# Moving a sums' buffer by 64 bytes and laying each row tile's activations side by side, in a hybrid decoder layer

## The chip, the cores and the metric

The kernel runs on one core of a Trainium2 chip. The metric is device time in microseconds (us); several runs of a kernel are taken and their median counts, and less is better. One more execution is recorded by the hardware profiler, and all rows of a profile come from that one.

## What is computed

One decoder layer on 1024 tokens of width 1024, all in float32:

```
h = rms_norm(x, mix_norm);  z = h @ w_in             # q, k, v, gates of two groups of heads
o_gla = gated linear attention, chunks of 64          # 4 heads
o_swa = sliding-window attention (128) with sinks     # 8 query heads, 2 kv heads
x  = x + concat([o_gla, o_swa]) @ w_out
h2 = rms_norm(x, ffn_norm)
u  = causal_depthwise_conv3(h2 @ w_up)                # 1024 -> 2 * 2816
a, b = split(u);  return x + (silu(a) * b) @ w_down   # 2816 -> 1024
```

## The kernel before

**Precision.** A float32 matmul is made of three fp32r matmuls. Each operand is split into a high part (index 0) and a rest (index 1), and the products high x high, high x rest and rest x high are summed in PSUM (`PASSES`). Every matmul is one weight load (128 columns of the stationary operand, `lhsT`) and one stream of up to 512 columns of the moving operand (`rhs`).

**Stages.** Tokens are cut into NT = 8 row tiles of 128, the model width into KD = 8 slices of 128. (1) `norm1` normalises a row tile and transposes it into the buffer `big` (`tr_hi` and `tr_lo` write the high part and the rest). (2) `dense` multiplies a row tile of `big` (stationary) by a block of w_in (moving): units dq, dk, dv, dg, dr, with the attention's small matmuls between them. (3) The gated outputs are written back into `big` (`gate_tr`), and `dense` multiplies them by w_out (do). (4) `norm2` normalises again; row tiles 0 to 3 go into `big` as before, and for tiles 4 to 7 `norm2_sums` forms sums and differences with tiles 0 to 3, which go into `big` and into the sums' buffer `ex`. (5) The gated MLP: DFF = 2816 is cut into 22 chunks of 128. For each chunk `product` does seven products of twelve matmuls each (a scheme after Strassen and Winograd, seven half-size products in place of eight): the stationary operand is a 128x128 piece of the chunk's w_up operand (A11w, A12w, S1w to S4w, A22w), the moving operand is 512 tokens of an activation, which `b_operand` picks: B11, B21, B22 and T1 lie in `big`, T2, T3 and T4 in `ex`. Between two products stands one `down_pair` (L1024), six matmuls of 512 columns for w_down, whose result VectorE adds to `acc` (L1028). At the end `last_row` does the last two chunks' share of w_down.

**Names in the profile.** `fb<-ex,S2w` at L843 is a product into a PSUM bank fb with moving operand in `ex` and stationary operand S2w; `gb<-` are those of chunk 0; `dn_P<-dw,dg` at L1024 is a `down_pair`.

**Order.** A list of times (`at`, `at_us`) sorts the steps once when the program is built; TensorE, VectorE, ScalarE and GpSimd then run their own rows in that order. An operand of `product` is made two products ahead by ScalarE (high part) and by GpSimd or VectorE (rest).

**Where buffers lie.** SBUF gives each of the 128 partitions the same byte addresses. Pools are stacked: from below `base` (`big`, raw weights, small things), upon it `gl` (attention), and once that is closed `acc`, then `ex`, then `pn` or `ff`; from above the nine weight slots of 4096 bytes (`slot_tile`), which hold all stationary operands of the products, and both operands of `down_pair`. Start addresses in bytes, from the program's allocation, with what is left modulo 256 (below: the phase):

| buffer | start before | phase before | phase after |
|---|---|---|---|
| weight slots (lowest 192384, steps of 4096) | 192384 | 128 | 128 |
| `big` | 1152 | 128 | 128 |
| `ex` | 112448 | 64 | 128 |
| A11w and A12w of chunk 1 (a pool above `ex`, not slots) | 178240, 182336 | 64 | 128 |
| `acc` | 79680 | 64 | 128 |
| kw, ident, qo, vg (from above) | | 0, 128, 128, 128 | the same |
| the attention's tiles in `gl` | | various | each 64 more |

Indices inside `big` and `ex` move by multiples of 512 bytes, so they keep the phase.

Of the kernel before, what the change touches and what calls it, by code (L numbers as in the profile page):

```python
# [9 lines left out]
F32 = mybir.dt.float32  # L10
F32R = mybir.dt.float32r
# [6 lines left out]
P = 128  # L18
T = 1024
D = 1024  # L20
NT = T // P
KD = D // P
# [12 lines left out]
def hymba_layer_kernel(ctx, tc, x, mix_norm, w_in, w_alpha2, b_alpha, gla_norm,  # L35
# [3 lines left out]
    act, dve, pool, pe, sp = nc.scalar, nc.vector, nc.gpsimd, nc.tensor, nc.sync  # L39
# [10 lines left out]
    base = ctx.enter_context(tc.tile_pool(name="base", bufs=1))  # L50
# [4 lines left out]
    def bank(name):  # L55
        ps["n"] += 1
        if "f" in ps:
            return ps["f"][2 + ps["n"] % 2]

        for start, which in (("n2pt_6", "b"), ("do1_7", "a"), ("n2pt_3", "a")):  # L60
            if name.startswith(start):
                return ps[which].tile([P, 512], F32, tag="b", name=name)
        return ps["ab"[ps["n"] % 2]].tile([P, 512], F32, tag="b", name=name)

    big = base.tile([P, 2, KD, 2, 4, P], F32R, name="big")

    def rows(t, ks, r):
        return big[:, t // 4, ks, r, t % 4, :]

    RAW_BUFS, K4, K2, N_WARM = 3, 6, 5, 5  # L70

# [23 lines left out]
    def split(src, hi, lo, eng=None, hi_eng=None):  # L95
        if hi_eng is None:
            act.copy(hi, src)  # L97
        else:
            hi_eng.tensor_copy(hi, src)
        (eng or pool).tensor_sub(lo, src, hi.bitcast(F32))  # L100
# [89 lines left out]
    def norm1_tr(t, i):  # L190
        tr_hi(t, i, xts["h", t], "n1")

    def norm1_lo(t, i):
        tr_lo(t, i, "n1")
# [32 lines left out]
    def norm2_sums(t):  # L227

        i, ex, pn = t - 4, fin["ex"], fin["pn"]
        p0, p1 = fin["pb", t]  # L230

        def put(src, hi, lo):
            split(src, hi, lo, dve)

        def extra(n):
            return ex[:, n, :, 0, i, :], ex[:, n, :, 1, i, :]

        def own(ks):
            return rows(t, ks, 0), rows(t, ks, 1)

        b12 = pn.tile([P, 4, P], F32, tag="b12", name=f"b12_{t}", bufs=1)
        b11, b21 = ([rows(i, ks, r).bitcast(F32) for r in range(2)] for ks in (slice(0, 4), slice(4, 8)))
        act.copy(b12, p0)
        put(p1, *own(slice(4, 8)))
        dve.tensor_sub(p0, p0, b11[0])
        dve.tensor_sub(p0, p0, b11[1])
        put(p0, *own(slice(0, 4)))
        dve.tensor_sub(p1, p1, b12)
        put(p1, *extra(1))
        dve.tensor_add(p1, p1, b11[0])  # L250
        dve.tensor_add(p1, p1, b11[1])
        put(p1, *extra(0))
        dve.tensor_sub(p0, b21[0], p1)
        dve.tensor_add(p0, p0, b21[1])
        put(p0, *extra(2))

    trs = {}

    def tr_hi(t, q, h, tag):
        pt = bank(f"{tag}pt_{t}_{q}")  # L260
        for k in range(4):
            c = (q * 4 + k) * P
            pe.transpose(pt[:, k * P:(k + 1) * P], h[:, c:c + P], ident)
        trs[tag, t, q] = pt.rearrange("p (k c) -> p k c", k=4)
        act.copy(rows(t, slice(q * 4, q * 4 + 4), 0), trs[tag, t, q])

    def tr_lo(t, q, tag):
        hi, lo = (rows(t, slice(q * 4, q * 4 + 4), r) for r in range(2))
        dve.tensor_sub(lo, trs[tag, t, q], hi.bitcast(F32))

    def norm_tr(t, h, tag):
        for q in range(2):
            tr_hi(t, q, h, tag)
            tr_lo(t, q, tag)


    blocks = {}
# [45 lines left out]
    def dense(t, ws, n, name):  # L323
        pb = bank(name)
        for k in range(KD):
            for i, (ra, rb) in enumerate(PASSES):
                pe.matmul(pb[:, :n], lhsT=rows(t, k, ra), rhs=ws[k][:, rb, :n],  # L327
                          start=(k == 0 and i == 0), stop=(k == KD - 1 and i == 2))
        return pb

# [299 lines left out]
    def gate_tr(t, gs):  # L630
        pb = bank(f"ogt{t}")
        for h in range(4):
            pe.transpose(pb[:, h * P:(h + 1) * P], gs[:, h * P:(h + 1) * P], ident)
        pv = pb.rearrange("p (h c) -> p h c", h=4)
        hi, lo = (rows(t, slice(0, 4), r) for r in range(2))
        act.activation(hi, pv, AF.Copy, scale=glan)
        dve.scalar_tensor_tensor(lo, pv, glan, hi.bitcast(F32), op0=ALU.mult, op1=ALU.subtract)
        src = qo[:, t, :].rearrange("p (j c) -> p j c", j=4)
        hi, lo = (rows(t, slice(4, 8), r) for r in range(2))
        split(src, hi, lo)  # L640


    fin = {}
# [19 lines left out]
    def open_norm2():  # L663
        st.close()
        w_late["pool"] = swp.enter_context(tc.tile_pool(name="wb", bufs=1, side="right"))
        xp = ctx.enter_context(tc.tile_pool(name="xp", bufs=1))
        fin["ex"] = xp.tile([P, 3, 4, 2, 4, P], F32R, name="ex")
        fin["sn"] = ExitStack()
        pn = fin["pn"] = fin["sn"].enter_context(tc.tile_pool(name="pn", bufs=1))
        ffn = fin["ffn"] = pn.tile([P, D], F32, name="ffn")  # L670
        sp.dma_start(ffn, ffn_norm.partition_broadcast(P).rearrange("p o d -> p (o d)"))
        fin["s1"] = pn.tile([P, 4, P], F32, name="s1_0")
# [18 lines left out]
    psb = {}  # L691
# [18 lines left out]
    def unit_q_part(t, k0, k1):  # L710
        if k0 == 0:
            psb["q", t] = bank(f"dq{t}")
        pb = psb["q", t]
        for k in range(k0, k1):

            for i, (ra, rb) in enumerate(((0, 0), (1, 0), (0, 1))):
                pe.matmul(pb, lhsT=rows(t, k, ra), rhs=blocks["q"][k][:, rb, :],  # L717
                          start=(k == 0 and i == 0), stop=(k == KD - 1 and i == 2))

    def q_done(t):  # L720
# [2 lines left out]
    def unit_q(t):  # L723
        q_post(t, dense(t, blocks["q"], 512, f"dq{t}"))

    def unit_k(t):
        kvl_post(t, dense(t, blocks["k"], 272, f"dk{t}"))

    def unit_v(t):
        act.activation(vg[0][:, t, :], dense(t, blocks["v"], 512, f"dv{t}"), AF.Copy, scale=row_scale(t))  # L730
# [78 lines left out]

    def b_operand(name, k, r):  # L810
        ex = fin["ex"]
        return {"B11": big[:, 0, k, r], "B21": big[:, 0, 4 + k, r],
                "B22": big[:, 1, 4 + k, r], "T1": big[:, 1, k, r],
                "T2": ex[:, 0, k, r], "T3": ex[:, 1, k, r], "T4": ex[:, 2, k, r]}[name]

    PROD = {"P1": ("A11", "B11"), "P2": ("A12", "B21"), "P3": ("S4", "B22"), "P4": ("A22", "T4"),
            "P5": ("S1", "T1"), "P6": ("S2", "T2"), "P7": ("S3", "T3")}
# [12 lines left out]
    def product(ch, name):  # L830
        an, bn = PROD[name]
        w = blocks["u", ch, an]
        onto = ONTO.get(name)
        if ch == 0 and name == "P3":
            onto = None
        if onto is None:
            psb[name, ch] = up_bank(ch, {"P1": 0, "P2": 1, "P3": 2, "P5": 2 if ch else 3}[name])
        pb = psb[name, ch] = psb[onto or name, ch]
        steps = [(k, ra, rb) for k in range(4) for ra, rb in PASSES]
        if ch == 0:  # L840
            steps.sort(key=lambda step: step[2])
        for i, (k, ra, rb) in enumerate(steps):
            pe.matmul(pb, lhsT=w[:, ra, k, :], rhs=b_operand(bn, k, rb),  # L843
                      start=(onto is None and i == 0), stop=(i == 11), skip_group_check=onto is not None)
# [50 lines left out]
        act.copy(dst, pb)  # L895

    def save_edge(ch, key, pb):
        e = psb[key, ch] = fin["ff"].tile([P, 2], F32, tag="e", name=f"{key}_{ch}", bufs=2)
        act.copy(e, pb[:, 510:512])

    def c11(ch):
# [196 lines left out]
    for c in halves:  # L1098
        split(mix_row[:, c], mix_hl[0][0:1, c], mix_hl[1][0:1, c], dve)
        pb = bank(f"mix{len(mix_ps)}")  # L1100
# [4 lines left out]
    def mix_copy():  # L1105
        for c, pb in zip(halves, mix_ps):
# [3 lines left out]
    TU = TO + 16.0  # L1110
    FIRST = ((norm1_mul, 0, 0), (q_hi, 0), (q_lo, 0, pool), (norm1_mul, 0, 1), (warm_up, 2), (norm1_tr, 0, 0),
             (norm1_lo, 0, 0), (q_hi, 1), (q_lo, 1, dve), (warm_up, 1), (norm1_tr, 0, 1), (warm_up, 2), (unit_q_part, 0, 0, 2), (q_hi, 2), (q_lo, 2, pool),
             (q_hi, 3), (norm1_mul, 1, 0), (q_lo, 3, dve), (unit_q_part, 0, 2, 3), (norm1_tr, 1, 0),
             (norm1_lo, 1, 0), (unit_q_part, 0, 3, 4), (q_hi, 4), (q_lo, 4, pool), (norm1_lo, 0, 1),
             (norm1_mul, 1, 1), (unit_q_part, 1, 0, 3), (q_hi, 5), (q_lo, 5, pool), (norm1_tr, 1, 1),
             (unit_q_part, 1, 3, 4), (norm1_lo, 1, 1), (q_hi, 6), (q_lo, 6, dve), (q_hi, 7), (q_lo, 7, pool),
# [80 lines left out]
    at(TO + 8.006, mark)  # L1197
    at(TO - 0.05, open_acc)
    at(TO + 1.35, open_norm2)
    def at_us(us, f, *a):  # L1200
        at(TU + us / 5.2, f, *a)
# [18 lines left out]
    for ch, i, name in order:  # L1220
# [7 lines left out]
        if ch < 2 or (ch, i) == (2, 0):  # L1228
            n = 0
        elif ch < L - 1 or (ch, i) == (L - 1, 0):  # L1230
            n = 1
        else:
            n = 2
# [24 lines left out]
    for p in range(NPAIR):  # L1258
        for k in range(7):

            n = 7 * p + k - 2
# [51 lines left out]
```

## Time and profile before

| | |
|---|---|
| runs | median 1039.2 us of 3 (1038.97 to 1039.4) |
| profiled execution, its own time | 1039.1 us |
| its span, first to last instruction | 1037.4 us |
| granted TensorE clock over the span | 1.000 |
| TensorE matmuls | busy 99% of the span, 4976 instructions |
| VectorE, GpSimd, ScalarE | busy 76%, 60%, 46% of the span |

How to read it: the span is what the rows add up to; 1.7 us of the execution lie around it. A group's row gives line, engine, operation, output<-inputs, shape and count, then busy time and the mean duration of one. Matmuls are pipelined: the duration of one runs from its start to its modelled end and is longer than the distance from one start to the next, so what a matmul costs in a dense stretch is read from the starts in the timeline.

### The profile page before, as it was taken

To read this page: it belongs to the slowest core of one execution; us is meant where nothing else is said; L and a number is where in the kernel's file an instruction comes from. 1 tells how busy PE (TensorE), PEld (TensorE's weight loads), DVE (VectorE), ACT (ScalarE), POOL (GpSimd) and SP (SyncE) were. 2 spreads that over 40 slices of the span, in tenths; PEclk is the share of its full clock that TensorE was granted. 3 is DMA by queue.
4 is the path that set the end of the run, shared out by engine and by line. 5 is a ranking of instruction groups with operands and counts; after the bars stand their busy time and mean duration, and the time that the engine had idled before them with its cause. 6 is when DMAs were issued, how large, how long until landed. Compare 5 with 4: busy or idle time off the path is not lost.

```text
span 1037.4 us, 13921 instructions
## 1 busy us (share of the span) xinstructions
PE 1030.0 (99%) x4976; PEld 849.3 (82%) x4976; DVE 793.4 (76%) x1332; ACT 480.6 (46%) x988; POOL 618.4 (60%) x510
## 2 busy tenths in 40 slices
PE   9999999999999999999999999999999999999998
PEld 6899887888888888888888888888888888888887
DVE  6776667755131699887979899897979798998976
ACT  5627655445340446554444445444444444454441
POOL 4592132325550205867868787877778787978750
PEclk9999999999999999999999999999999999999999
DMA  6152113002044202112120111222121211121104
GB/s 217 61 154 62 45 50 93 21 1 82 1 122 163 61 1 82 41 41 82 41 81 26 57 45 57 61 62 62 41 82 41 62 41 47 55 62 61 41 21 162
DMA packets 67502, 67.13 MB, mean 65 GB/s; under 512 B 4648, under 2 KB 52201, under 8 KB 67434
## 3 DMA queue, kind: packets, MB, share of 16 engines
q1 hardware_dynamic: 63448, 61.27, 18.9%
q10 hardware_dynamic: 3986, 4.99, 2.0%
q8 instruction: 39, 0.64, 0.2%
q14 instruction: 29, 0.24, 0.1%
HBM read 57.33 MB, written 4.19 MB: 59 GB/s over the span
## 4 chain that ended last, share of the span: by engine, by line
PE 97%; DMA 1%; DVE 1%; ACT 0%; issue 0%; POOL 0%; DVEq 0%; ACTq 0%; SPq 0%
PE fb L843 39%; PE dn_P L1024 18%; PE do L327 8%; PE dr L327 4%; PE dg L327 4%; PE dv L327 4%; PE dq L327 3%; PE dk L327 2%; PE gb L843 2%; PE dq L717 1%; PE pv L500 1%; PE fb L1053 1%; PE dl L1053 1%; PE go L610 1%; PE ga L601 1%; PE sc L453 1%
## 5 line engine op out<-in xcount | busy, mean ns | idle before, releaser
L1028 DVE TENSOR_TENSOR acc<-acc,dn_P 128x1024 f32<-128x1024 f32 x140 | 169.9, 1215 | 61.5 <-PE dn_P L1024 60.3
L1024 PE MATMUL dn_P<-dw,dg 128*128 128x512 f32 x840 | 214.0, 390 | 0.0
L1024 PEld LDWEIGHTS dn_P<-dw,dg 128*128 128x128 f32 x840 | 157.6, 188 | 34.5
L327 PE MATMUL do<-wow,big 128*128 128x512 f32 x384 | 90.9, 393 | 0.0
L100 POOL TENSOR_TENSOR dw<-dn,dw 128x512 fp32r<-128x512 f32 x50 | 68.8, 1376 | 25.3 <-ACT dw L97 24.1
L327 PEld LDWEIGHTS do<-wow,big 128*128 128x128 f32 x384 | 71.1, 188 | 14.4
L895 ACT COPY ca<-fb 128x512 f32<-128x512 f32 x62 | 36.3, 586 | 68.2 <-PE fb L843 68.2
L843 PE MATMUL fb<-ex,S2w 128*128 128x512 f32 x252 | 62.5, 394 | 0.0
L843 PE MATMUL fb<-ex,S3w 128*128 128x512 f32 x252 | 62.5, 394 | 0.0
L850 DVE SCALAR_TENSOR_TENSOR ua<-fb,cc,ua 128x511 f32<-128x511 f32 x84 | 62.2, 741 | 0.3
L843 PE MATMUL fb<-ex,A22w 128*128 128x512 f32 x252 | 62.2, 394 | 0.0
L843 PE MATMUL fb<-big,A11w 128*128 128x512 f32 x252 | 61.2, 389 | 0.0
L843 PE MATMUL fb<-big,S1w 128*128 128x512 f32 x252 | 61.1, 389 | 0.0
L843 PE MATMUL fb<-big,S4w 128*128 128x512 f32 x252 | 61.1, 389 | 0.0
L843 PE MATMUL fb<-big,A12w 128*128 128x512 f32 x252 | 60.9, 390 | 0.0
L843 PEld LDWEIGHTS fb<-ex,S2w 128*128 128x128 f32 x252 | 47.2, 187 | 11.3
L843 PEld LDWEIGHTS fb<-ex,A22w 128*128 128x128 f32 x252 | 47.2, 187 | 11.3
L843 PEld LDWEIGHTS fb<-ex,S3w 128*128 128x128 f32 x252 | 47.2, 187 | 11.3
L843 PEld LDWEIGHTS fb<-big,S1w 128*128 128x128 f32 x252 | 47.3, 188 | 10.0
L843 PEld LDWEIGHTS fb<-big,A11w 128*128 128x128 f32 x252 | 47.3, 188 | 10.0
L843 PEld LDWEIGHTS fb<-big,S4w 128*128 128x128 f32 x252 | 47.3, 188 | 10.0
L843 PEld LDWEIGHTS fb<-big,A12w 128*128 128x128 f32 x252 | 47.2, 188 | 9.8
(432 smaller groups left out, 2392.1 us busy)
## 6 DMA issues: line engine op xcount, KB each, us to landing
up<-in_w_up_dram SPq DMA_DIRECT2D x44, 512.0 KB, 3.8
dn<-in_w_down_dram SPq DMA_DIRECT2D x22, 512.0 KB, 3.5
acc<-in_x_dram SPq DMA_DIRECT2D x8, 512.0 KB, 6.5
out_dram<-acc SPq DMA_DIRECT2D x15, 256.0 KB, 2.0
xt<-in_x_dram SPq DMA_DIRECT2D x7, 512.0 KB, 3.2
vraw<-in_w_in_dram SPq DMA_DIRECT2D x4, 512.0 KB, 3.9
graw<-in_w_in_dram SPq DMA_DIRECT2D x4, 512.0 KB, 3.7
qt<-qt ACTq DMA_DIRECT2D x16, 128.0 KB, 2.2
```

The lines of the kernel that those rows point to most:

```text
L100: (eng or pool).tensor_sub(lo, src, hi.bitcast(F32))
L327: pe.matmul(pb[:, :n], lhsT=rows(t, k, ra), rhs=ws[k][:, rb, :n], start=(k == 0 and i == 0), stop=(k == KD - 1 and i == 2))
L453: pe.matmul(pbs[-1][:, j % 2, :], lhsT=ql[:, g, qc], rhs=kt[:, g, kc], start=False, stop=True)
L500: pe.matmul(pbs[i][HALF[g]], lhsT=vv[rows, t - 1 + b, HALF[g]], rhs=rhs[rows, :, HALF[i]], start=start, stop=stop)
L601: pe.matmul(pb[:, pr * 256:(pr + 1) * 256], lhsT=gqt[t][:, pr, :], rhs=qbd[t % 2][:, pr], start=(pr == 0), stop=(pr == 1))
L610: pe.matmul(pb[:, h * P:(h + 1) * P], lhsT=asb[:, h, :], rhs=v[:, h * P:(h + 1) * P], start=(h == 0), stop=(t == 0 and h == 3))
L843: pe.matmul(pb, lhsT=w[:, ra, k, :], rhs=b_operand(bn, k, rb), start=(onto is None and i == 0), stop=(i == 11), skip_group_check=onto is n ...
L850: dve.scalar_tensor_tensor(dst, src, w, dst, op0=ALU.mult, op1=ALU.add)
L895: act.copy(dst, pb)
L1024: pe.matmul(pb[:, i], lhsT=g[:, ra, c:c + P], rhs=w[:, rb, :], start=(onto is None and n == 0), stop=(n == 2), skip_group_check=onto is no ...
L1028: dve.tensor_add(acc, acc, pb)
L1053: pe.matmul(pb[:, c0:c1], lhsT=g[:, ra, (t % 4) * P:(t % 4 + 1) * P], rhs=w[:, rb, c0:c1], start=(ch == NCH - 2 and i == 0), stop=(ch == N ...
```

## The change

Two things, and no instruction is added, removed or moved: both programs issue the same instructions on every engine in the same order. What differs is addresses and access patterns.

First, the two tiles of `save_edge` (`e`, [128, 2], the last two token rows of a half) come from `base` and no longer from `ff`. `base` grows by two buffers of 32 bytes, and all that is stacked above it starts 64 bytes higher; in `ff` the tiles behind the old place of `e` stay where they were.

Second, the index order of `big` and of `ex`. Before, the 512 tokens of four row tiles lay side by side for each slice k and part r: the moving operand of a product was one run of 2048 bytes in each partition, and the eight slices of one row tile lay 4096 bytes apart, high part and rest 2048 bytes apart. Afterwards a row tile's slices and parts lie side by side: the moving operand of a product is four runs of 512 bytes, 8192 bytes apart in `big` and 4096 bytes apart in `ex`; a row tile's slices are 1024 bytes apart, high part and rest 512. A stationary operand taken from `big` is one run of 512 bytes either way.

```diff
-    big = base.tile([P, 2, KD, 2, 4, P], F32R, name="big")
-
-    def rows(t, ks, r):
-        return big[:, t // 4, ks, r, t % 4, :]
+    big = base.tile([P, NT, KD, 2, P], F32R, name="big")
...
-        act.copy(rows(t, slice(q * 4, q * 4 + 4), 0), trs[tag, t, q])
+        act.copy(big[:, t, q * 4:q * 4 + 4, 0, :], trs[tag, t, q])
...
-                pe.matmul(pb[:, :n], lhsT=rows(t, k, ra), rhs=ws[k][:, rb, :n],
+                pe.matmul(pb[:, :n], lhsT=big[:, t, k, ra, :], rhs=ws[k][:, rb, :n],
...
-        fin["ex"] = xp.tile([P, 3, 4, 2, 4, P], F32R, name="ex")
+        fin["ex"] = xp.tile([P, 3, 4, 4, 2, P], F32R, name="ex")
...
-        return {"B11": big[:, 0, k, r], "B21": big[:, 0, 4 + k, r],
-                "B22": big[:, 1, 4 + k, r], "T1": big[:, 1, k, r],
-                "T2": ex[:, 0, k, r], "T3": ex[:, 1, k, r], "T4": ex[:, 2, k, r]}[name]
+        return {"B11": big[:, 0:4, k, r, :], "B21": big[:, 0:4, 4 + k, r, :],
+                "B22": big[:, 4:8, 4 + k, r, :], "T1": big[:, 4:8, k, r, :],
+                "T2": ex[:, 0, :, k, r, :], "T3": ex[:, 1, :, k, r, :],
+                "T4": ex[:, 2, :, k, r, :]}[name]
...
-        e = psb[key, ch] = fin["ff"].tile([P, 2], F32, tag="e", name=f"{key}_{ch}", bufs=2)
+        e = psb[key, ch] = base.tile([P, 2], F32, tag="e", name=f"{key}_{ch}", bufs=2)
```

The other lines of the diff (`norm2_sums`, `tr_lo`, `gate_tr`, `unit_q_part`) only write the new indices.

More of the change, by code (lines that the diff above doesn't have):

```diff
@@ L230, in norm2_sums, with put @@
         p0, p1 = fin["pb", t]
[L232 to L239, printed above, removed]
+        def put(src, dst):
+            split(src, dst[:, :, 0, :], dst[:, :, 1, :], dve)
         b12 = pn.tile([P, 4, P], F32, tag="b12", name=f"b12_{t}", bufs=1)
-        b11, b21 = ([rows(i, ks, r).bitcast(F32) for r in range(2)] for ks in (slice(0, 4), slice(4, 8)))
+        b11, b21 = big[:, i, 0:4].bitcast(F32), big[:, i, 4:8].bitcast(F32)
         act.copy(b12, p0)
[L244 to L247, printed above, removed]
+        put(p1, big[:, t, 4:8])
+        dve.tensor_sub(p0, p0, b11[:, :, 0, :])
+        dve.tensor_sub(p0, p0, b11[:, :, 1, :])
+        put(p0, big[:, t, 0:4])
         dve.tensor_sub(p1, p1, b12)
[L249 to L255, printed above, removed]
+        put(p1, ex[:, 1, i])
+        dve.tensor_add(p1, p1, b11[:, :, 0, :])
+        dve.tensor_add(p1, p1, b11[:, :, 1, :])
+        put(p1, ex[:, 0, i])
+        dve.tensor_sub(p0, b21[:, :, 0, :], p1)
+        dve.tensor_add(p0, p0, b21[:, :, 1, :])
+        put(p0, ex[:, 2, i])
     trs = {}
@@ L264, in tr_hi @@
         trs[tag, t, q] = pt.rearrange("p (k c) -> p k c", k=4)
-        act.copy(rows(t, slice(q * 4, q * 4 + 4), 0), trs[tag, t, q])
+        act.copy(big[:, t, q * 4:q * 4 + 4, 0, :], trs[tag, t, q])
     def tr_lo(t, q, tag):
-        hi, lo = (rows(t, slice(q * 4, q * 4 + 4), r) for r in range(2))
+        hi, lo = big[:, t, q * 4:q * 4 + 4, 0, :], big[:, t, q * 4:q * 4 + 4, 1, :]
         dve.tensor_sub(lo, trs[tag, t, q], hi.bitcast(F32))
@@ L634, in gate_tr @@
         pv = pb.rearrange("p (h c) -> p h c", h=4)
-        hi, lo = (rows(t, slice(0, 4), r) for r in range(2))
+        hi, lo = big[:, t, 0:4, 0, :], big[:, t, 0:4, 1, :]
         act.activation(hi, pv, AF.Copy, scale=glan)
@@ L638, in gate_tr @@
         src = qo[:, t, :].rearrange("p (j c) -> p j c", j=4)
-        hi, lo = (rows(t, slice(4, 8), r) for r in range(2))
+        hi, lo = big[:, t, 4:8, 0, :], big[:, t, 4:8, 1, :]
         split(src, hi, lo)
@@ L716, in unit_q_part @@
             for i, (ra, rb) in enumerate(((0, 0), (1, 0), (0, 1))):
-                pe.matmul(pb, lhsT=rows(t, k, ra), rhs=blocks["q"][k][:, rb, :],
+                pe.matmul(pb, lhsT=big[:, t, k, ra, :], rhs=blocks["q"][k][:, rb, :],
                           start=(k == 0 and i == 0), stop=(k == KD - 1 and i == 2))
```

## The prediction

> **What bounds the kernel now.** I read the page from the top: busy shares, then the chain that ended last, then the costliest groups.
>
> ```profile
> span 1037.4 us, 13921 instructions
> PE 1030.0 (99%) x4976; PEld 849.3 (82%) x4976; DVE 793.4 (76%) x1332; ACT 480.6 (46%) x988; POOL 618.4 (60%) x510
> ...
> PE 97%; DMA 1%; DVE 1%; ACT 0%; issue 0%; POOL 0%; DVEq 0%; ACTq 0%; SPq 0%
> ...
> L1028 DVE TENSOR_TENSOR acc<-acc,dn_P 128x1024 f32<-128x1024 f32 x140 | 169.9, 1215 | 61.5 <-PE dn_P L1024 60.3
> L1024 PE MATMUL dn_P<-dw,dg 128*128 128x512 f32 x840 | 214.0, 390 | 0.0
> ...
> L843 PE MATMUL fb<-ex,S2w 128*128 128x512 f32 x252 | 62.5, 394 | 0.0
> L843 PE MATMUL fb<-ex,S3w 128*128 128x512 f32 x252 | 62.5, 394 | 0.0
> ...
> L843 PE MATMUL fb<-ex,A22w 128*128 128x512 f32 x252 | 62.2, 394 | 0.0
> L843 PE MATMUL fb<-big,A11w 128*128 128x512 f32 x252 | 61.2, 389 | 0.0
> L843 PE MATMUL fb<-big,S1w 128*128 128x512 f32 x252 | 61.1, 389 | 0.0
> ...
> L843 PE MATMUL fb<-big,A12w 128*128 128x512 f32 x252 | 60.9, 390 | 0.0
> ```
>
> TensorE is the bound: 97% of the chain, and the product groups have no idle time ahead of them (the last column is 0.0). What one matmul costs is therefore what the kernel costs. The rows to look at twice are those of L843: the same shape, the same nine slots for the stationary operands, and yet 394 ns where the moving operand lies in `ex` and 389 to 390 where it lies in `big`. The medians, and the twelve further matmuls of chunk 0 (gb), say the same, in a view of line 843 with minimum, median and maximum:
>
> ```profile
> L843 PE MATMUL fb<-ex,S2w x252: 393/394/398, 414.2 to 995.1; 128*128 128x512 f32 x126
> L843 PE MATMUL fb<-big,S1w x252: 388/389/398, 420.7 to 1008.9; 128*128 128x512 f32 x126
> L843 PE MATMUL gb<-ex,A22w x12: 394/394/394, 423.4 to 426.0; 128*128 128x512 f32 x12
> ```
>
> The spread is a few ns over 580 us, so this is no contention with other engines, which would vary; it belongs to the addresses. The timeline of TensorE gives the price from start to start (columns: start, length, engine, group):
>
> ```profile
> 701.18 2.96 PE L843 MATMUL fb<-ex,S2w 128*128 128x512 f32 x12
> 703.98 1.54 PE L1024 MATMUL dn_P<-dw,dg 128*128 128x512 f32 x6
> 705.36 2.88 PE L843 MATMUL fb<-big,S1w 128*128 128x512 f32 x12
> 708.08 1.52 PE L1024 MATMUL dn_P<-dw,dg 128*128 128x512 f32 x6
> 709.44 2.96 PE L843 MATMUL fb<-ex,S3w 128*128 128x512 f32 x12
> ...
> 730.04 2.96 PE L843 MATMUL fb<-ex,S2w 128*128 128x512 f32 x12
> ```
>
> A product from `ex` takes 703.98 - 701.18 = 2.80 us, one from `big` 708.08 - 705.36 = 2.72: 233.3 and 226.7 ns a matmul. The unit behind a product from `ex` takes 705.36 - 703.98 = 1.38, the one behind `big` 709.44 - 708.08 = 1.36: after `ex` the stream needs some matmuls to get back into step. The whole cycle of a chunk, from S2w to S2w, is 730.04 - 701.18 = 28.86 us, and seven products and seven units at 2.72 and 1.36 would be 28.56: the difference of 0.30 is three times (0.08 + 0.02), so nothing else is lost there.
>
> Is it the phase? `ex` starts at 64 modulo 256 and everything else in these rows at 128, so two explanations fit: the phase, or something else about `ex`. One place tells them apart. The operands A11w and A12w of chunk 1 don't lie in slots but at phase 64, while their moving operand is `big`:
>
> ```profile
> 399.48 2.46 PE L843 MATMUL fb<-big,A11w 128*128 128x512 f32 x10
> 401.77 1.08 PE L843 MATMUL gb<-big,A12w 128*128 128x512 f32 x4
> ```
>
> and, among the matmuls that write fb between 399 and 407 us, with minimum, median and maximum:
>
> ```profile
> L843 PE MATMUL fb<-big,A12w x12: 388/394/477, 403.7 to 406.3; 128*128 128x512 f32 x12
> L843 PE MATMUL fb<-big,A11w x11: 388/392/397, 399.5 to 402.7; 128*128 128x512 f32 x11
> ```
>
> (401.77 - 399.48) / 10 = 229 ns, medians 392 and 394: with the stationary operand 64 bytes off and `ex` not involved, matmuls are slow as well. So it is the difference between the two operands' phases, and I take equal phases for worth 226.7.
>
> **The change, part by part.**
>
> *`ex` at phase 128.* Products from `ex`: 3 x 252 + 3 x 12 = 792 matmuls, 66 products. At 0.08 each that is 66 x 0.08 = 5.28 us. The getting back into step, 0.02, falls away behind each of them but some four in chunks 0 and 1 where one product from `ex` follows another: 62 x 0.02 = 1.24. All of it lies on TensorE with no idle time, so all of it counts. Sum 6.5.
>
> *A11w and A12w of chunk 1 at phase 128.* 24 matmuls at 229 - 226.7 = 2.3 ns: 0.06 us, lost in rounding.
>
> *The moving operand in four runs.* All 7 x 252 + 7 x 12 = 1848 product matmuls now read 4 x 128 elements with three jumps. No fp32r matmul of this kernel does so; the nearest are plain float32 ones, 256 columns in four runs of 64 (L500) against 256 in one run (L420):
>
> ```profile
> L500 PE MATMUL pv<-pt,vv x120: 376/379/431, 119.0 to 253.8; 128*64 128x256 f32 x64, 64*64 64x256 f32 x56
> ...
> L420 PE MATMUL za<-wa,gt x16: 377/379/382, 79.4 to 114.4; 128*128 128x256 f32 x16
> ```
>
> Both have a median of 379: three jumps cost nothing there. I take 0, since jumps of 4096 and 8192 bytes leave the phase as it is and each run is two whole periods of 256. The row is weak, as a plain float32 matmul takes in its columns more slowly. The other end: if every matmul lost in the jumps what a foreign phase costs it, 6.7 ns, it would be 1848 x 6.7 = 12.3 us. A gain I exclude: the undisturbed rows of `big`, dn_P and the rest all stand at 389 to 390.
>
> *Row tiles side by side, as stationary operands.* `dense` reads runs of 512 bytes, before and after, at multiples of 512; only the distance from one to the next falls, from 2048 or more to 512. The weight loads of dn_P already have 512-byte neighbours, those of do are spread out, and both take 188 ns:
>
> ```profile
> L1024 PEld LDWEIGHTS dn_P<-dw,dg 128*128 128x128 f32 x840 | 157.6, 188 | 34.5
> ...
> L327 PEld LDWEIGHTS do<-wow,big 128*128 128x128 f32 x384 | 71.1, 188 | 14.4
> ```
>
> So 0. ScalarE's and VectorE's writes into `big` and `ex` stay four runs of 512 bytes at another distance; they are off the chain, and I cost them at 0 under TensorE's cover.
>
> *64 bytes for the attention's tiles.* In the first 394 us `dense` does not run quite at its best:
>
> ```profile
> L327 PE MATMUL do<-wow,big 128*128 128x512 f32 x384 | 90.9, 393 | 0.0
> ...
> L327 PE MATMUL dg<-gw,big 128*128 128x512 f32 x192 | 47.0, 399 | 1.0 <-ACT vg L730 1.0
> L327 PE MATMUL dv<-vw,big 128*128 128x512 f32 x192 | 46.5, 395 | 0.0
> L327 PE MATMUL dr<-rw,big 128*128 128x512 f32 x192 | 46.5, 396 | 0.0
> ```
>
> Above 389 that is 384 x 4 + 192 x (10 + 6 + 7) ns = 6.0 us, waits and getting into step after each small matmul. The phases of `big` and the slots don't move; those of the small matmuls between them do, together, so each keeps its neighbours in `gl` in phase. I take 0; a shift of a sixth of the 6.0, 1 us, either way goes into the range.
>
> *What comes due earlier.* The chunk shrinks to 28.56 us, and the other engines must keep up. Busy time in 440 us of this stage (PE, PEld, DVE, ACT, POOL):
>
> ```profile
> 560.00:1000.00 440.00, 440.00 (x1923) 360.20 (x1922) 388.91 (x482) 210.07 (x357) 341.72 (x251) 1.00 0.18 54
> ```
>
> VectorE goes from 388.91 / 440 = 88% to 388.91 / 435.4 = 89%, and the L1028 row shows it waiting 60.3 us for dn_P: it stays behind TensorE.
>
> The sum is 6.5 us against the profiled execution: 1039.1 - 6.5 = 1032.6. The median of the runs lies 0.1 above that execution: 1032.7.
>
> **The rivals.**
>
> *The jumps cost* (slower). In every product each matmul loses one step of 6.7 ns at its jumps, and `ex` gains what it gains: 1032.7 + 12.3 = 1045.0. It decides from 6.5 us / 1848 = 3.5 ns a matmul on. For it: no fp32r row with jumps exists, and a stream that falls out of step by 64 bytes pays. Against it: L500 beside L420, and jumps by whole periods. 0.13. With 2.4 to 4.6 ns the two parts would cancel within 2.1 us: 0.02, and with less the kernel is still faster: 0.02.
>
> *The phase is not what makes `ex` slow* (no change): 1039.2. For it: every row at 394 has `ex` in it, and the chunk 1 rows are only 24 matmuls, some next to transposes. The Trainium skill, "TensorE: Matmul & The Clock Gate", section "Step-by-step: what each phase is for", says that the moving operand and the weight load have read ports of their own, so that loading weights takes nothing from the running matmul; by that rule the distance of two addresses could not matter, and the time would stay at 1039.2. The trace disagrees in that 2.80 and 2.72 differ by the operands' places alone. 0.07.
>
> *VectorE or GpSimd becomes the bound.* Excluded by the 88% and 341.72 / 440 = 78% above as long as the order stays.
>
> **How the numbers follow.** Forecast 0.76, its own range 1031.5 (6.5 + 0.1, and the 1 us in `dense`) to 1034.0 (without the 1.24, or with that 1 us). Jumps that cost: 0.13 slower, 0.02 cancelling, 0.02 at some 1036. Phase without effect: 0.07. This measurement tells about 0.2%, 2.1 us, from no change: faster 0.76 + 0.02 = 0.78, same 0.02 + 0.07 = 0.09, slower 0.13. The range of 8 in 10 reaches from 1031.5 to the cases without effect, 1039.4, and leaves the slower ones out.
>
> **What would show it.** Right: the `ex` groups of L843 at 389, products of 2.72 and units of 1.36 throughout, S2w to S2w 28.56, a span of 1030.9, `dense` as before. If the `big` groups rise above 389, the jumps cost; if `ex` stays at 394 at phase 128, the phase was not the cause; if the gain is there but `dense` has moved, it is the shift of `gl`. The forecast is wrong as soon as jumps cost 3.5 ns.

## The result and the profile after

The kernel after takes 1032.99 us (median of 4, 1032.79 to 1033.26) against 1039.28 before (median of 4): a ratio of 0.994, 95% interval 0.9923 to 0.9957. The forecast was 1032.7. The profiled execution took 1033.08 us, its span is 1031.4. Its page, head and costliest groups (line numbers are 8 to 9 lower than before):

```profile
span 1031.4 us, 13921 instructions
PE 1023.9 (99%) x4976; PEld 849.5 (82%) x4976; DVE 795.6 (77%) x1332; ACT 480.7 (47%) x988; POOL 618.3 (60%) x510
...
L1016 PE MATMUL dn_P<-dw,dg 128*128 128x512 f32 x840 | 212.9, 389 | 0.0
...
L318 PE MATMUL do<-wow,big 128*128 128x512 f32 x384 | 90.9, 393 | 0.0
...
L835 PE MATMUL fb<-big,A12w 128*128 128x512 f32 x252 | 60.9, 390 | 0.2 <-DVE ua L842 0.2
...
L835 PE MATMUL fb<-big,S1w 128*128 128x512 f32 x252 | 61.0, 389 | 0.0
L835 PE MATMUL fb<-ex,S3w 128*128 128x512 f32 x252 | 60.9, 389 | 0.0
```

Every fb group of products now stands at 389 to 390, `ex` and `big` alike; dn_P has come down from 390 to 389, and `do` is where it was. The timeline of TensorE over one chunk:

```profile
698.20 2.88 PE L835 MATMUL fb<-ex,S2w 128*128 128x512 f32 x12
700.92 1.52 PE L1016 MATMUL dn_P<-dw,dg 128*128 128x512 f32 x6
702.28 2.88 PE L835 MATMUL fb<-big,S1w 128*128 128x512 f32 x12
...
726.76 2.88 PE L835 MATMUL fb<-ex,S2w 128*128 128x512 f32 x12
```

A product from `ex` takes 700.92 - 698.20 = 2.72 us and the unit behind it 702.28 - 700.92 = 1.36, and from S2w to S2w it is 726.76 - 698.20 = 28.56 us. These are the three numbers of the forecast, to the hundredth.

The span fell by 6.0 us, 0.5 less than the 6.5. The missing half microsecond stands at two places where TensorE now waits for VectorE. The one is seen at the A12w row above (0.2, ended by DVE ua), and the timeline of the two engines shows both:

```profile
436.61 2.88 PE L835 MATMUL fb<-big,A11w 128*128 128x512 f32 x12
438.88 0.73 DVE L842 SCALAR_TENSOR_TENSOR ua<-fb,cc,ua 128x510 f32<-128x510 f32 x1
439.67 3.01 PE L835 MATMUL fb<-big,A12w 128*128 128x512 f32 x12 [0.18 <-DVE ua L842]
442.52 2.88 PE L835 MATMUL fb<-ex,S2w 128*128 128x512 f32 x12
```

```profile
962.26 1.21 DVE L1020 TENSOR_TENSOR acc<-acc,dn_P 128x1024 f32<-128x1024 f32 x1
962.95 0.61 PE L835 MATMUL fb<-big,S1w 128*128 128x512 f32 x2
963.52 1.65 PE L1016 MATMUL dn_P<-dw,dg 128*128 128x512 f32 x6
965.01 2.22 PE L835 MATMUL fb<-ex,S3w 128*128 128x512 f32 x9
```

At 436.61 the product takes 439.67 - 436.61 = 3.06 us, 0.34 more than 2.72, and the next 442.52 - 439.67 = 2.85, 0.13 more: in chunk 2 a PSUM bank comes free only when VectorE has read it for chunk 1 (438.88 + 0.73 = 439.61), and TensorE arrives earlier than before. At 962.95 two matmuls and a unit take 965.01 - 962.95 = 2.06 us for eight matmuls, where 8 x 0.2267 = 1.81 would do: 0.25 more. VectorE's addition of an earlier unit to `acc` ends at 962.26 + 1.21 = 963.47, and the unit starts behind it, at 963.52. Together 0.7 us, part of which is the stream getting back into step after the wait.

The stage of the products can be read by itself, from the first product (394.56 before, 394.42 after) to the start of the last `last_row` group (1033.02 and 1026.99): 638.46 us before, 632.57 after, 5.9 less. That is the 6.5, less the 0.7, and the 0.06 of A11w and A12w of chunk 1. The other 0.14 lies ahead of the first product and is not shown to come from the change: in the profiled executions of the runs below that keep the weight slots and `big` in phase with each other, the first product starts anywhere from 394.21 to 395.04.

### The profile page after: what moved, and what is told of

It reads as the page before. It is cut to its first block, busy times and chain, and to the rows that moved or that the text cites. A ratio compares the mean times of both kernels' runs of the same rounds, so it can differ in the third digit from the quotient of the medians.

```text
span 1031.4 us, 13921 instructions
## 1 busy us (share of the span) xinstructions
PE 1023.9 (99%) x4976; PEld 849.5 (82%) x4976; DVE 795.6 (77%) x1332; ACT 480.7 (47%) x988; POOL 618.3 (60%) x510
## 4 chain that ended last, share of the span: by engine, by line
PE 96%; DVE 2%; ACT 1%; DMA 0%; issue 0%; POOL 0%; ACTq 0%; SPq 0%
PE fb L835 38%; PE dn_P L1016 18%; PE do L318 8%; PE dg L318 4%; PE dr L318 4%; PE dv L318 4%; PE dq L318 3%; PE dk L318 2%; PE gb L835 2%; PE dq L708 1%; PE pv L491 1%; PE dl L1045 1%; PE fb L1045 1%; PE go L601 1%; PE ga L592 1%; PE sc L443 1%
```

## The experiments

The theory: what counts is the difference of the start addresses of the moving and the stationary operand modulo 256 bytes; four runs in place of one, and the new place of row tiles, neither cost nor bring anything.

**The phase alone.** The kernel before, with the edge tiles moved and all index orders left.

```diff
-        e = psb[key, ch] = fin["ff"].tile([P, 2], F32, tag="e", name=f"{key}_{ch}", bufs=2)
+        e = psb[key, ch] = base.tile([P, 2], F32, tag="e", name=f"{key}_{ch}", bufs=2)
```

> The kernel before with only the two edge tiles moved into the pool below the sums' buffer: ex, A11w_1 and A12w_1 at phase 128 like the weight slots, moving operands still one run of 2048 bytes. Theory (the phase is all of it): products from ex take 2.72 us instead of 2.80 and the units behind them 1.36 instead of 1.38; 1039.2 - 6.3 = 1032.9 us, the same as the whole change within 0.5. Rival (the new index order brings part of the gain): above 1033.5, up to 1039.2 if it brings all.

Measured: 1032.91 us, ratio 0.9944 (0.993 to 0.9957). The groups:

```profile
L843 PE MATMUL fb<-big,A12w 128*128 128x512 f32 x252 | 61.0, 390 | 0.2 <-DVE ua L850 0.2
L843 PE MATMUL fb<-ex,S3w 128*128 128x512 f32 x252 | 60.9, 389 | 0.0
```

The one moved line does all of it, down to the wait of A12w for VectorE. The rival that the index order brings part of the gain falls.

**The index order alone.** The kernel after, with the edge tiles back in `ff`.

```diff
-        e = psb[key, ch] = base.tile([P, 2], F32, tag="e", name=f"{key}_{ch}", bufs=2)
+        e = psb[key, ch] = fin["ff"].tile([P, 2], F32, tag="e", name=f"{key}_{ch}", bufs=2)
```

> The whole change with the edge tiles put back into their old pool: four runs of 512 bytes, ex back at phase 64. Theory (the index order costs and brings nothing): products from big 2.72, from ex 2.80, units 1.36 and 1.38; 1039.2 us within 0.7. Rival (jumps cost a little that the phase's gain hid): 1840 products' matmuls times the cost, so 1040.0 us already at 0.5 ns each. Rival (four runs remove the penalty of a foreign phase too): about 1033.

Measured: 1039.51 us, ratio 1.0002 (0.9993 to 1.0011). A view of the products' line:

```profile
L835 PE MATMUL fb<-ex,S2w x252: 393/394/398, 414.6 to 995.6; 128*128 128x512 f32 x126
...
L835 PE MATMUL fb<-big,S1w x252: 388/389/398, 421.2 to 1009.4; 128*128 128x512 f32 x126
```

These are the rows of before, though both groups now read four runs. The interval leaves room for 1.1 us over 1848 matmuls with three jumps each, 0.6 ns a matmul; the slower rival needed 3.5. The timeline leaves less. The first product and the last `last_row` group:

```profile
395.04 2.11 PE L835 MATMUL gb<-big,A11w 128*128 128x512 f32 x8 [0.24 <-ACT big L256]
...
1033.51 0.87 PE L1045 MATMUL fb<-dnw,g 128*128 128x256 f32 x6
```

The stage takes 1033.51 - 395.04 = 638.47 us, against 638.46 in the kernel before. With `ex` at phase 128 it is 632.57 with one run (the phase alone, 394.91 to 1027.48) and 632.57 with four (the kernel after). So the jumps cost nothing that these traces could show, with `ex` in phase or out of it, and the four runs don't take the penalty of a foreign phase away.

**All slots moved by 64 bytes.** From the kernel after; the right-hand tiles, the slots among them, start at phase 192, `big` and `ex` stay at 128.

```diff
-    mhalf = edge.tile([P, 24], F32, name="mhalf")
+    mhalf = edge.tile([P, 8], F32, name="mhalf")
```

> The whole change with a constant tile at the top cut from 24 to 8 columns, so that all weight slots start 64 bytes higher, phase 192, while big and ex stay at 128: now every product has its moving operand 64 bytes below its stationary one, as ex had before, and the dense units have the moving operand 64 bytes above. Theory (the difference of phases counts): all 154 products 2.80 and each unit behind them 1.38, 154 x 0.10 = 15.4 us, and in the dense units 229 instead of 226.7 ns as with A11w of chunk 1, some 1100 x 2.3 = 2.6 us: 1033 + 18 = 1051 us. Rival (it was something else about ex, or the absolute address): 1033 us.

Measured: 1047.93 us, ratio 1.0089 (1.0075 to 1.0103). Groups, and the timeline over one product from each buffer:

```profile
L1016 PE MATMUL dn_P<-dw,dg 128*128 128x512 f32 x840 | 215.5, 392 | 0.0
L318 PE MATMUL do<-wow,big 128*128 128x512 f32 x384 | 91.5, 395 | 0.0
...
L835 PE MATMUL fb<-big,S1w 128*128 128x512 f32 x252 | 62.7, 394 | 0.0
...
L835 PE MATMUL fb<-ex,S2w 128*128 128x512 f32 x252 | 62.5, 394 | 0.0
```

```profile
705.92 2.96 PE L835 MATMUL fb<-ex,S2w 128*128 128x512 f32 x12
708.72 1.54 PE L1016 MATMUL dn_P<-dw,dg 128*128 128x512 f32 x6
710.10 2.96 PE L835 MATMUL fb<-big,S1w 128*128 128x512 f32 x12
712.90 1.54 PE L1016 MATMUL dn_P<-dw,dg 128*128 128x512 f32 x6
```

Now `big` is as slow as `ex` was: products 2.80 (708.72 - 705.92 and 712.90 - 710.10), the unit 1.38. The two operands of dn_P moved together and it loses only the getting into step. The theory's 18 us came out as 15. The first product starts at 395.39 for 394.42, so the dense units lost about 1 us in place of 2.6 (`do` went from 393 to 395, others less; why they lose less than A11w of chunk 1 did is not shown). From the first product on it is 14.0 us more in place of 15.4: the waits for VectorE vanish in a slower stream (0.7), the units are 140 and not 154 (0.3), and A11w and A12w of chunk 1, which don't lie in slots, stay at phase 128 like `big` (0.2); what remains is 0.2. That the kernel is 8.7 us slower than before, and 14.9 slower than the kernel after, shows that `ex` as such was never the cause.

**Everything moved by 64 bytes.** As the last, and ahead of `big` an unused tile:

```diff
+    base.tile([P, 16], F32, name="pad")
     big = base.tile([P, NT, KD, 2, P], F32R, name="big")
```

> As the run with the slots at phase 192, and an unused tile of 64 bytes ahead of big, so that big and ex start at 192 too. Theory (only the difference counts): 1033.0 us within 0.7, products 2.72 and units 1.36. Rival (the absolute phase 128 counts): all products slow, about 1050 us.

Measured: 1032.84 us, ratio 0.9941 (0.9928 to 0.9955), the time of the kernel after.

```profile
L836 PE MATMUL fb<-big,S1w 128*128 128x512 f32 x252 | 61.0, 389 | 0.0
...
L836 PE MATMUL fb<-ex,S2w 128*128 128x512 f32 x252 | 60.9, 389 | 0.0
```

With all three at 192 the products are at 389 again: the difference counts, the absolute phase doesn't.

**The price by phase.** A kernel that computes nothing of the layer: groups of 48 matmuls with one stationary and one moving buffer that start at the same phase, and offsets given by the group.

```diff
+    for d in range(16):
+        group("one_" + LET[d], runs(4 * d, 1, 0))            # moving operand d * 16 bytes further
+    for n, step, key in ((4, 1024, "four"), (4, 1040, "fourq"), ...):
+        group(key, runs(0, n, step))                          # n runs, step elements apart
+    group("stq", runs(0, 1, 0), soff=16)                      # stationary operand 64 bytes further
```

> None of the layer is computed: groups of 48 matmuls of 512 columns with one stationary buffer (128 columns each, its places 512 bytes apart), and the moving operand moved by 0, 16, 32 ... 240 bytes (groups one_a to one_p); then four runs of 128 elements with steps that keep the phase (four) or shift it by 64, 128 or 16 bytes a run (fourq, fourh, fours), 8 to 64 runs, two groups of 256 columns, and the stationary operand moved instead (stq, sth, stt) or both (both). Theory (only the difference of phases modulo 256 counts, whole-period jumps are free): one_a 226.7 ns from start to start, one_m (192 bytes ahead, that is 64 below) 233.3, the rest between 226 and 240 and periodic in 256; four, eight as one_a, both as one_a, stq as one_m, stt (192 ahead) as one_e. Rival (jumps cost): four above one_a by a ns or more. Rival (a fixed 16-cycle step whenever phases differ): all of one_b to one_p at 233.3.

TensorE's timeline (start, length from the first start to the modelled end of the last); (length - 11.04) / 48 is the price against equal phases, as a mean over a group, the first matmuls that get into step included. All groups come from one execution:

```profile
25.08 11.04 PE L82 MATMUL one_a<-mv,st 128*128 128x512 f32 x48
35.96 11.28 PE L82 MATMUL one_b<-mv,st 128*128 128x512 f32 x48
...
69.48 11.16 PE L82 MATMUL one_e<-mv,st 128*128 128x512 f32 x48
...
113.87 11.32 PE L82 MATMUL one_i<-mv,st 128*128 128x512 f32 x48
...
158.66 11.35 PE L82 MATMUL one_m<-mv,st 128*128 128x512 f32 x48
...
192.31 11.05 PE L82 MATMUL one_p<-mv,st 128*128 128x512 f32 x48
203.20 11.08 PE L82 MATMUL four<-mv,st 128*128 128x512 f32 x48
214.12 11.67 PE L82 MATMUL fourq<-mv,st 128*128 128x512 f32 x48
...
248.02 11.05 PE L82 MATMUL eight<-mv,st 128*128 128x512 f32 x48
258.91 11.52 PE L82 MATMUL sixteen<-mv,st 128*128 128x512 f32 x48
...
306.23 5.91 PE L82 MATMUL thin_a<-mv,st 128*128 128x256 f32 x48
311.98 5.82 PE L82 MATMUL thin_q<-mv,st 128*128 128x256 f32 x48
317.63 11.36 PE L82 MATMUL stq<-mv,st 128*128 128x512 f32 x48
...
350.99 11.06 PE L82 MATMUL both<-mv,st 128*128 128x512 f32 x48
```

From one_a to one_b start to start it is (35.96 - 25.08) / 48 = 226.7 ns: equal phases give the best that the kernel's products reach. Moving operand 64 bytes above (one_e): 2.5 ns more; 64 below (one_m): 6.5; the stationary one 64 above (stq): 6.7; both moved: 0.4. The asymmetry of the kernel, 229 against 233.3, is thus in the two operands alone. The rival of one fixed step falls: one_b costs 5 ns, one_e 2.5, one_i (128) 5.8, and 16 bytes below (one_p) nothing. Four runs whose steps keep the phase cost 0.04 us over 48 matmuls, all of it in the first nine, from one start to the next; behind them it is 226 to 227 ns as with one run. Eight runs cost 0.01. Four runs whose phase shifts by 64 bytes each (fourq) cost 13 ns, and sixteen runs of 32 elements 10 ns although their steps are whole periods: runs of 128 and 64 elements were free, 32 are not. One pair goes the other way: with 256 columns the group that lies 64 bytes above (thin_q) is not dearer than the one in phase (thin_a) but cheaper, 5.82 against 5.91, some 2 ns a matmul. What is said here of the price holds for 512 columns.

**The period.** The same kernel with other offsets.

```diff
+    for key, off in (("per_a", 64), ("per_b", 128), ("per_c", 80), ("per_d", 48), ("per_e", 1024)):
+        group(key, runs(off, 1, 0))                           # off elements of 4 bytes
```

> None of the layer is computed: groups of 48 matmuls as in the phase curve. per_a, per_b, per_e: moving operand 256, 512 and 4096 bytes further than the stationary one's phase; per_c and per_d: 256 + 64 and 256 - 64. Theory (period 256): per_a, per_b, per_e 226.7 ns from start to start, per_c 228.9, per_d 233.3, as one_a, one_e and one_m. Rival (the period is longer, 512 or more): per_a off 226.7. low_h to low_a: 32, 24, 20, 16, 12, 8 and 4 bytes below; up_a to up_c: 4, 8 and 12 above. From the phase curve: 16 below is 226.7 and 32 below 233.3, 16 above 231.7; what lies between isn't known. n_a to n_h: 128, 192, 272, 320, 384, 448, 480 and 496 columns in phase: columns / 2.4 + 13.3 ns if the 13.3 ns above 512 / 2.4 = 213.3 belong to every matmul. still: the same 128 stationary columns each time: 226.7, or less if the 13.3 ns come from the change of stationary place.

```profile
24.14 11.04 PE L82 MATMUL per_a<-mv,st 128*128 128x512 f32 x48
...
45.91 11.17 PE L82 MATMUL per_c<-mv,st 128*128 128x512 f32 x48
56.91 11.35 PE L82 MATMUL per_d<-mv,st 128*128 128x512 f32 x48
...
112.32 11.04 PE L82 MATMUL low_d<-mv,st 128*128 128x512 f32 x48
123.20 11.68 PE L82 MATMUL low_c<-mv,st 128*128 128x512 f32 x48
...
156.66 11.52 PE L82 MATMUL up_a<-mv,st 128*128 128x512 f32 x48
...
253.34 11.07 PE L82 MATMUL still<-mv,st 128*128 128x512 f32 x48
```

256 bytes further (per_a) is as good as 0, 256 + 64 (per_c) as 64, 256 - 64 (per_d) as 64 below: the period is 256 bytes; that it is no shorter one that divides 256 was shown by the one_i row (128 bytes, 5.8 ns). Between the multiples of 16 bytes the price is not smooth: 16 below (low_d) is free, 12 below (low_c) costs 13 ns, 4 above (up_a) 10. A stationary operand that is the same 128 columns each time (still) is no cheaper than places that change: 11.07, 0.03 more for getting into step. Of the groups of fewer columns those of 272, 320 and 384 cost what was expected; 448 to 496 cost 3 to 7 ns more, and 128 and 192 some 111 ns each where 67 and 93 were expected, so the 13.3 ns don't belong to every matmul alike. This kernel's products have 512.

## Why the prediction was right

*TensorE bounds and the products cost what they cost.* Right. *`ex` at phase 128 gains 0.08 a product and 0.02 in the unit behind.* Right to the hundredth in the timeline, and shown as the cause by the phase alone (1032.91), by its reversal (1047.93) and by moving everything (1032.84). The count of 62 units with 0.02 was near enough: the stage as a whole gave the 6.5 but for the waits below.

*The argument for the phase, from two dozen matmuls of chunk 1.* It held. Those rows have become 389 as well, among the matmuls that write fb between 399 and 406 us of the kernel after:

```profile
L835 PE MATMUL fb<-big,A12w x12: 389/389/476, 403.5 to 406.1; 128*128 128x512 f32 x12
L835 PE MATMUL fb<-big,A11w x11: 389/389/393, 399.3 to 402.5; 128*128 128x512 f32 x11
```

That `ex` was slow by its own nature, the rival of no change, was refuted by `big` at 394 with the slots moved. The Trainium skill's rule of separate read ports ("TensorE: Matmul & The Clock Gate", section "Step-by-step: what each phase is for") does not cover this: here the price depends on the two addresses together (one_m and stq 6.5 and 6.7 ns, both 0.4).

*Four runs cost 0.* Right, and the weak row from plain float32 was not needed: the index order alone gave 1.0002 and a stage of the same length, the group of four 0.04 us over 48. The choice of 0 rested on jumps and runs of whole periods, and both mattered: with shifting phases (fourq) it would have been 13 ns a matmul, and with runs of 32 elements, half a period, 10.

*Row tiles side by side cost 0, the shift of `gl` about 0.* Right: `do` 393 before and after, first product at 394.56 and 394.42, a difference smaller than that between profiled executions.

*VectorE stays behind.* Mis-sized. Read over 440 us it does, but not at every place: at 439.7 and 963.5 TensorE waits for it, 0.7 us in all, and that is why the span fell by 6.0 and not 6.5. An average of 88% over hundreds of us hides a single chunk. That the median still came within 0.3 of the forecast, 1032.99 for 1032.7, is in part luck: the median of the kernel before had moved from 1039.2 to 1039.28, and the runs of the kernel after spread over 0.5 us.

## What to carry to other kernels

Where matmuls of one shape differ by a constant few ns between operand buffers, with hardly any spread over the whole run, compare the buffers' start addresses with those of the stationary operands modulo 256 bytes; here 64 bytes of one small tile were worth 0.6%. All of that was measured with fp32r matmuls of 512 columns; the one pair of 256 columns went the other way. An index order of the moving operand was free with runs of 64 and 128 elements of four bytes and steps that keep the phase, so among such orders it can be chosen for other reasons. And the stream that got faster everywhere met VectorE first at single places, which the average over the stage had hidden.

## What was not expected of the hardware

The price has no simple law in the offset: free at 0 and at 16 bytes below, 13 ns at 12 below, 10 at 4 above, 2.5 at 64 above, 6.5 at 64 below. It is a steady rhythm, not a delay once: in the kernel before, the matmuls of a product from `ex` start 233 to 234 ns apart throughout. And it takes some matmuls to leave it: in the unit behind such a product the distances are 226, 236, 228, 233, 231 and 226 ns, 1380 in place of 1360, which is why that unit paid too. What in the chip makes the rhythm is not shown by these runs. None of them beats the kernel after: the moved line alone (1032.91) and everything moved (1032.84) lie within its own spread.
